# Dense-token operands written to DRAM by the routing step instead of transposed again by the dense step

## The chip, the core and the metric

The kernel runs on one core of one Trainium2 chip. The metric is the device time of one execution in microseconds (us), taken as the median of several runs. A further execution is recorded by the hardware profiler, and all durations below are from that one.

## What is computed

One layer of a transformer over 1024 latent tokens (8 blocks of 128) with 256 context tokens, width 1024. After a mixing half (retention and differential attention, not touched here) comes the expert half:

```python
x = x + mod[:, 2] * (jnp.concatenate([ret_lat, diff_lat], axis=-1) @ w_out[layer])
h2 = modulate(x, norm2_g[layer], mod[:, 3], mod[:, 4])
x = x + mod[:, 5] * peer_ffn(h2, peer_w_query[layer], peer_sub_keys[layer], peer_u[layer], peer_v[layer])

def block_fn(hb):                       # 128 tokens of h2
    q = (hb @ w_query).reshape(t, PEER_HEADS, 2, PEER_HALF)
    s = jnp.einsum('thpc,hpnc->thpn', q, sub_keys)
    v1, i1 = lax.top_k(s[:, :, 0], PEER_TOPK)
    v2, i2 = lax.top_k(s[:, :, 1], PEER_TOPK)
    ...
    u, vsel = expert_u[experts], expert_v[experts]
    act = jax.nn.gelu(jnp.einsum('thkd,td->thk', u, hb), approximate=False)
    return jnp.einsum('thk,thkd->td', gate * act, vsel)
```

Each token picks 16 of 16384 experts in each of 8 heads (routing) and adds up their outputs with gates.

## The kernel before

**Blocks.** The eight token blocks are mixed in five groups, `GROUPS = [[0], [4, 5], [6, 7], [3], [1, 2]]`. For each group, `mix` (attention, output projection, residual, second norm) leaves the normalised tokens `x1` in buffers of tag `b` (four buffers) and writes them to DRAM (`h2d[b]`). `route` then transposes the group's tokens on TensorE with the identity (`mm<-ident,b`), copies them to tiles `hts` (also tag `b`), and for each of the 8 heads loads the query weights (`wst<-w_query_chunks`, two of the four `wst` buffers), multiplies (`mm<-b,wst`), copies the queries (`u<-mm`), scores them against the keys (`mm<-sk,u`), and finds the 16 best on VectorE (`vi`, `s`), twice per block and head (once for each half key). `select` combines them.

**Two ways of evaluating the experts.** Blocks 0, 1 and 2 gather expert rows with indirect DMAs (`halves`: `gat<-peer_u`, `gat<-peer_v`, and a VectorE operation for each). Blocks `DENSE = [3, 4, 5, 6, 7]` (640 tokens) go through all 16384 experts in `dense_phase`. For these, `gates` first writes a table of gate values to DRAM (`Wd`): one unit of four tokens is a VectorE pair, four ScalarE operations `t<-ob,pt`, four TensorE multiplications `mm<-t,t` and four ScalarE copies (`rv<-mm` or `gat<-mm`). There are 160 units.

**The dense operands.** Products run as three multiplications of rounded halves (`three`), so the tokens are needed transposed, as a high half (five tiles of tag `k`) and a low half (five tiles of tag `v`), each 128 by 1024:

```python
ts = [sb([128, 1024], tag, F32R) for _ in range(5)]
wide = [ts[k // 2][:, k % 2 * 384:(k % 2 + 1) * 384] for k in range(KD)]
thin = [ts[k][:, 768:1024] if k < 4 else ts[4][:, (k - 4) * 256:(k - 3) * 256] for k in range(KD)]
```

`wide` holds blocks 3, 4, 5, `thin` blocks 6, 7. The same buffers hold keys and values of the attention until the last group has been mixed. `split_tokens` fills them: it loads `h2d` of each dense block (tag `b`), transposes it again (8 transposes for a block), and for each 128 by 128 piece ScalarE rounds the high half from PSUM and VectorE subtracts for the low half. Then `dense_act` loads the experts' columns (`wst<-peer_u_cols`), splits them (`h<-wst`, ScalarE then VectorE) and multiplies (`mm<-k,h`, `mm<-v,h`), and after four of these `dense_val` multiplies with the experts' output rows (`mm<-h,rv`, `mm<-h,t`).

**The order of the work.** Nothing is issued as it is written. Every operation is recorded as a node (all instructions therefore carry line L591, a helper's). Parts that shall overlap are interleaved by `weave`, which places operation j of n of a part at a fraction `lo + (hi - lo) * j / n`; the last weave joins `gates` of block 3, `dense_phase`, and `route` of blocks 1 and 2. Then `Plan.schedule` simulates the engines and the buffers by a table of costs and picks, on each engine, the ready node of lowest priority number whose buffers are free. It runs seven times with adjusted priorities, and the best order is built. So a change of one part's length or of its dependences can move instructions anywhere after it.

Of the kernel before, what the change touches and what calls it, by code (L numbers as in the profile page):

```python
# [6 lines left out]
F32 = mybir.dt.float32  # L7
# [5 lines left out]
OP = mybir.AluOpType  # L13
AX = mybir.AxisListType

D = 1024
# [5 lines left out]
KD = D // 128  # L22
# [38 lines left out]
DENSE = [3, 4, 5, 6, 7]  # L61
ND = 128 * len(DENSE)
RANGES = [(0, 384), (384, 640)]
# [534 lines left out]
def layer(tc, I, out, dbg=None):  # L598
# [3 lines left out]
    with sp as S, pp as P, dp as DR:  # L602
# [9 lines left out]
        nc = Plan(tc, pools, bufs, {"mm": RESERVE})  # L612

        def eng(pattern, i):
            return nc.gpsimd if pattern[i % len(pattern)] == "P" else nc.vector

        def sb(shape, tag, dt=F32):
            return nc.tile(shape, dt, tag)

        def ps(shape):  # L620
            return nc.tile(shape, F32, "mm")

        def dr(shape, name):
            return nc.tile(shape, F32, name, dram=True)

        def dump(name, sl, t):
            if dbg is not None and name in dbg:
                nc.sync.dma_start(dbg[name][sl], t)


        ident = sb([128, 128], "ident")
# [19 lines left out]
        def rstd(dst, mean):  # L651

            n = mean.free
            nc.vector.tensor_scalar(dst, mean, EPS, None, op0=OP.add)
            nc.gpsimd.tensor_tensor(out=dst, in0=dst, in1=mhalf[:, :n], op=OP.pow)
# [24 lines left out]
        def wstream(src, c0):  # L680

            w = []
            for i in range(2):
                t = sb([128, 4, 256], "wst")
                nc.sync.dma_start(t, src[c0 // 256, :, i * 4:(i + 1) * 4, :])
                w += [t[:, k, :] for k in range(4)]
            return w
# [103 lines left out]
        for a in range(2):  # L791
            nc.vector.tensor_tensor(out=dec[:, a], in0=cols[:, a, :, None].to_broadcast([128, 4, H]),
                                    in1=lg[:, a:a + 1, :].to_broadcast([128, 4, H]), op=OP.mult)
# [303 lines left out]
        def mod_row(i):  # L1097
            t = sb([128, D], "h")
            nc.sync.dma_start(t, modr[i:i + 1, :].to_broadcast([128, D]))
            return t  # L1100
# [6 lines left out]
        h2d = [dr([128, D], f"h2d{b}") for b in range(NB)]  # L1107
# [78 lines left out]
        def mix(grp):  # L1186

            cT = []
            for b in grp:
                attend(b, cT)  # L1190
            x1 = [sb([128, D], "b") for _ in grp]
            gate1 = mod_row(0)
            for ch in range(4):
                w = wstream(wo, ch * 256)
                for i, b in enumerate(grp):
                    pm = ps([128, 256])
                    with nc.unit():
                        for k in range(KD):
                            nc.tensor.matmul(pm, cT[i][:, k, :], w[k], start=(k == 0), stop=(k == KD - 1))
                    cs = slice(ch * 256, (ch + 1) * 256)  # L1200
                    nc.vector.tensor_tensor(out=x1[i][:, cs], in0=pm, in1=gate1[:, cs], op=OP.mult)
            shift2, gs2 = mod_row(1), mod_row(2)
            for i, b in enumerate(grp):
                xr = sb([128, D], "wst")
                nc.sync.dma_start(xr, I["x"][0, b * 128:(b + 1) * 128, :])
                eng(XE, b).tensor_tensor(out=x1[i], in0=x1[i], in1=xr, op=OP.add)
                nc.sync.dma_start(x1d[b], x1[i])
                dump("x1", (slice(b * 128, (b + 1) * 128), slice(None)), x1[i])
                ms = sb([128, 2], "m4")
                nc.scalar.activation(xr, x1[i], AF.Square, scale=1.0 / 32.0, accum_out=ms[:, 0:1])  # L1210
                rstd(ms[:, 1:2], ms[:, 0:1])
                nc.vector.scalar_tensor_tensor(x1[i], x1[i], ms[:, 1:2], gs2, op0=OP.mult, op1=OP.mult)
                eng(XE, b).tensor_tensor(out=x1[i], in0=x1[i], in1=shift2, op=OP.add)
                nc.sync.dma_start(h2d[b], x1[i])
                dump("h2", (slice(b * 128, (b + 1) * 128), slice(None)), x1[i])
            return x1

        def top16(i, h, qT, sk, v16, i16):
            pm = ps([128, 2, 128])
            for s in range(2):  # L1220
                nc.tensor.matmul(pm[:, s, :], qT[s][:, i, :], sk[:, s, :], start=True, stop=True)
            s0 = sb([128, 2, 128], "u3")
            nc.scalar.copy(s0, pm)
            for s in range(2):
                s1 = sb([128, 128], "s1")
                vv, ii = v16[:, h, s, :], i16[:, h, s, :]
                nc.vector.max(vv[:, 0:8], s0[:, s, :])
                nc.vector.max_index(ii[:, 0:8], vv[:, 0:8], s0[:, s, :])
                nc.vector.match_replace(s1, vv[:, 0:8], s0[:, s, :], LOWEST)
                nc.vector.max(vv[:, 8:16], s1)  # L1230
                nc.vector.max_index(ii[:, 8:16], vv[:, 8:16], s1)

        def route(grp, x1):
            T = len(grp)
            kpt = KD // T
            hts = [sb([128, kpt, T, 128], "b") for _ in range(T)]
            for i, b in enumerate(grp):
                for g in range(KD // 4):
                    tp = ps([128, 4, 128])
                    with nc.unit():  # L1240
                        for q in range(4):
                            k = g * 4 + q
                            nc.tensor.transpose(tp[:, q, :], x1[i][:, k * 128:(k + 1) * 128], ident)
                    k0 = (g * 4) % kpt
                    nc.scalar.copy(hts[g * 4 // kpt][:, k0:k0 + 4, i, :], tp)
            vi = [sb([128, 2, PH, 2, TK], "vi") for _ in grp]
            v16, i16 = [t[:, 0] for t in vi], [t[:, 1].bitcast(U32) for t in vi]
            for h in range(PH):
                w = wstream(wq, h * 256)
                sk = sb([128, 2, 128], "sk")  # L1250
                nc.sync.dma_start(sk, I["peer_keys_cols"][h])
                qT = []
                for s in range(2):
                    pm = ps([128, T * 128])
                    with nc.unit():
                        for k in range(KD):
                            nc.tensor.matmul(pm, w[k][:, s * 128:(s + 1) * 128],
                                             hts[k // kpt][:, k % kpt].rearrange("p t c -> p (t c)"),
                                             start=(k == 0), stop=(k == KD - 1))
                    q = sb([128, T, 128], "u0" if s else "u4")  # L1260
                    nc.scalar.copy(q.rearrange("p t c -> p (t c)"), pm)
                    qT.append(q)
                for i in range(T):
                    top16(i, h, qT, sk, v16[i], i16[i])
            for i, b in enumerate(grp):
                select(b, v16[i], i16[i])

        def split_tokens():

            parts = []  # L1270
            for tag in ("k", "v"):
                ts = [sb([128, 1024], tag, F32R) for _ in range(5)]
                wide = [ts[k // 2][:, k % 2 * 384:(k % 2 + 1) * 384] for k in range(KD)]
                thin = [ts[k][:, 768:1024] if k < 4 else ts[4][:, (k - 4) * 256:(k - 3) * 256] for k in range(KD)]
                parts.append([wide, thin])
            for i, b in enumerate(DENSE):
                x = sb([128, D], "b")
                nc.sync.dma_start(x, h2d[b])
                f = 0 if i < 3 else 1
                cs = slice(i * 128 - RANGES[f][0], (i + 1) * 128 - RANGES[f][0])  # L1280
                for g in range(KD // 2):
                    tp = ps([128, 2, 128])
                    with nc.unit():
                        for q in range(2):
                            k = g * 2 + q
                            nc.tensor.transpose(tp[:, q, :], x[:, k * 128:(k + 1) * 128], ident)
                    for q in range(2):
                        h_, l_ = (t[f][g * 2 + q][:, cs] for t in parts)
                        nc.scalar.copy(h_, tp[:, q, :])
                        nc.vector.tensor_tensor(out=l_, in0=tp[:, q, :], in1=h_.bitcast(F32), op=OP.subtract)  # L1290
            return parts

        def select(b, v16, i16):
# [257 lines left out]
        def Q(g):  # L1551
            return C(route, GROUPS[g], x1s[g])
# [8 lines left out]
        for i in range(1, len(GROUPS) + 1):  # L1561
            assert LATE[min(i, len(LATE)) - 1] >= sum(map(len, GROUPS[1:i + 1]))
            q = Q(i - 1)
            last = i == len(GROUPS)
            parts = [] if last else [(q, *QSPAN[i - 1]), (A(i), *ASPAN[i - 1])]
# [76 lines left out]
```

## Time and profile before

| | us |
|---|---|
| median of 3 runs (lowest, highest) | 3334.67 (3334.27, 3337.14) |
| the profiled execution's own time | 3333.26 |
| its span, first to last instruction | 3331.5 |
| TensorE (PE) busy | 3088.1 (93%) |
| VectorE (DVE) busy | 2635.5 (79%) |
| ScalarE (ACT) busy | 1341.7 (40%) |
| GpSimd (POOL) busy | 1146.8 (34%) |

Shares are of the span. The engines work side by side, so the busy times don't add up; what a stage costs is read from the waits in that stage. Matmuls are pipelined: a group of n reads shorter, divided by n, than the mean of one. A float32 multiplication of the program stands in the trace as two matmul records, a transpose and a product of rounded halves as one. PEclk is the clock granted to TensorE, 1.00 being 2.4 GHz and 0.50 being 1.2 GHz.

### The profile page before, as it was taken

The page shows a single profiled execution, that of the slowest core. Times are in us where ns is not written, and L with a number is a line of the kernel's source. Part 1 is how long each engine was busy: PE and PEld are TensorE (multiplying, and loading weights), DVE is VectorE, ACT ScalarE, POOL GpSimd, SP SyncE. Part 2 cuts the span into 40 slices and gives each one's busy share as a digit, 9 for nine tenths or more (in the row PEclk, how much of TensorE's full clock was granted, in tenths as well). Part 3 has the DMA queues.
Part 4 walks back from the last instruction along what each step waited for, and adds up shares of the span by engine and source line. Part 5 has one row for each costly group of instructions (what it writes and reads, how often), then busy time and mean ns, then how long its engine had stood idle before and what let it go on. Part 6 is the DMA issues. An engine that isn't in the chain of part 4 may idle for free.

```text
span 3331.5 us, 51447 instructions
## 1 busy us (share of the span) xinstructions
PE 3088.1 (93%) x18272; PEld 2710.2 (81%) x18272; DVE 2635.5 (79%) x5951; ACT 1341.7 (40%) x3553; POOL 1146.8 (34%) x1099
## 2 busy tenths in 40 slices
PE   6998887878888898899999999999999999999998
PEld 4998576656767786788889898989898988999897
DVE  3457547879988988578988887888888887889895
ACT  5342454424356899883322222222222222222221
POOL 0101111453441201103545453454445443545440
PEclk7999998989989999999999999999999999999999
DMA  5222655886586553646888888888889887888883
GB/s 187 96 78 76 231 187 186 280 316 229 196 276 204 196 184 108 213 157 220 307 308 290 308 293 293 282 307 300 306 296 313 303 298 274 296 307 300 303 295 121
DMA packets 314531, 809.68 MB, mean 243 GB/s; under 512 B 29313, under 2 KB 125593, under 8 KB 314274
## 3 DMA queue, kind: packets, MB, share of 16 engines
q1 hardware_dynamic: 203682, 403.70, 35.9%
q0 software_dynamic: 110592, 402.70, 34.7%
q8 instruction: 144, 2.36, 0.3%
q14 instruction: 113, 0.93, 0.1%
HBM read 745.46 MB, written 60.83 MB: 242 GB/s over the span
## 4 chain that ended last, share of the span: by engine, by line
PE 54%; DVE 10%; ACT 6%; issue 3%; DMA 2%; POOL 1%; DVEq 0%; POOLq 0%; SPq 0%; ACTq 0%
PE mm L591 54%; ACT t L591 2%; DVE sel L591 2%; DVE acc L591 2%; ACT rv L591 1%; DVE gat L591 1%; DVE t L591 1%; ACT gat L591 1%; DVE h L591 1%; DMA gat<-peer_v,egb 1%; POOL gat L591 1%; DVE vi L591 1%; ACT h L591 1%; DVE m L591 1%; DMA gat<-peer_u,egb 1%
## 5 line engine op out<-in xcount | busy, mean ns | idle before, releaser
L591 PE MATMUL mm<-k,h 128*128 128x384 f32 (+1 forms) x4096 | 918.5, 309 | 6.2 <-DVE h L591 4.7
L591 PEld LDWEIGHTS mm<-k,h 128*128 128x128 f32 x4096 | 697.5, 189 | 15.4 <-DVE h L591 5.4
L591 POOL DMA_INDIRECT gat<-peer_u,egb x368 | 474.0, 1288 | 555.4 <-DVE acc L591 341.4
L591 ACT CAST h<-wst 128x512 fp32r<-128x512 f32 (+1 forms) x384 | 286.0, 764 | 888.8 <-PE mm L591 854.1
L591 POOL DMA_INDIRECT gat<-peer_v,egb x377 | 463.5, 1229 | 521.8 <-DVE gat L591 267.5
L591 PE MATMUL mm<-v,h 128*128 128x384 f32 (+1 forms) x2048 | 630.6, 308 | 0.0
L591 PE MATMUL mm<-h,rv 128*128 128x512 f32 x2304 | 586.7, 395 | 2.6 <-DVE h L591 1.8
L591 PEld LDWEIGHTS mm<-h,rv 128*128 128x128 f32 x2304 | 422.9, 188 | 96.6 <-DVE h L591 2.6
L591 DVE SCALAR_TENSOR_TENSOR acc<-gat,act,acc 128x1024 f32<-128x1024 f32 x374 | 480.6, 1285 | 6.4 <-DMA gat<-peer_v,egb 5.0
L591 DVE TENSOR_TENSOR h<-wst,h 128x512 fp32r<-128x512 f32 (+1 forms) x384 | 329.8, 867 | 177.6 <-ACT h L591 91.2
L591 DVE SCALAR_TENSOR_TENSOR gat<-gat,h2t 128x1024 f32<-128x1024 f32 x368 | 450.5, 1229 | 17.5 <-DMA gat<-peer_u,egb 17.5
L591 PE MATMUL mm<-h,t 128*128 128x512 f32 (+1 forms) x1600 | 416.8, 391 | 1.8 <-DVE t L591 1.1
L591 PEld LDWEIGHTS mm<-v,h 128*128 128x128 f32 x2048 | 386.4, 189 | 8.4
L591 PEld LDWEIGHTS mm<-h,t 128*128 128x128 f32 x1600 | 295.1, 189 | 68.2 <-DVE t L591 2.4
L591 POOL TENSOR_TENSOR m<-m,mhalf 128x4 f32<-128x4 f32 (+1 forms) x78 | 73.0, 938 | 689.5 <-DVE m L591 674.4
L591 PE MATMUL mm<-b,wst 128*128 128x256 f32 (+1 forms) x1280 | 240.5, 343 | 2.5 <-DMA wst<-w_query_chunks 2.1
L591 PE MATMUL mm<-t,t 128*128 128x128 f32 x1280 | 193.6, 298 | 45.0 <-ACT t L591 38.5
L591 ACT ACTIVATE t<-ob,pt 128x128 f32<-128x128 bf16 x640 | 220.1, 419 | 21.5 <-DVE ob L591 10.7
L591 PEld LDWEIGHTS mm<-b,wst 128*128 128x128 f32 x1280 | 206.2, 194 | 27.3 <-DMA wst<-w_query_chunks 2.7
L591 PEld LDWEIGHTS mm<-t,t 128*128 128x128 f32 x1280 | 173.4, 198 | 67.3 <-ACT t L591 58.4
L591 DVE TENSOR_TENSOR b<-b,mm 128x512 f32<-128x512 f32 x248 | 165.8, 682 | 61.5 <-PE mm L591 60.9
L591 PE MATMUL mm<-t,h 128*128 128x256 f32 x992 | 187.2, 286 | 6.2 <-DVE aT L591 2.8
(239 smaller groups left out, 4454.2 us busy)
## 6 DMA issues: line engine op xcount, KB each, us to landing
wst<-peer_u_cols SPq DMA_DIRECT2D x128, 512.0 KB, 7.3
wst<-peer_v_halves SPq DMA_DIRECT2D x128, 512.0 KB, 4.7
wst<-w_query_chunks SPq DMA_DIRECT2D x80, 512.0 KB, 5.7
h<-Wd SPq DMA_DIRECT2D x64, 512.0 KB, 7.8
wst<-w_mod_chunks SPq DMA_DIRECT2D x48, 512.0 KB, 5.1
wst<-w_out_chunks SPq DMA_DIRECT2D x40, 512.0 KB, 5.4
Wd<-rv SPq DMA_DIRECT2D x40, 512.0 KB, 3.6
Wd<-gat SPq DMA_DIRECT2D x40, 512.0 KB, 4.7
```

The lines of the kernel that those rows point to most:

```text
L591: getattr(handles[n.eng], meth)(*[res(v) for v in a], **k)
```

## The change

`route` additionally writes the transposed tokens of the dense blocks, which it holds in `hts` for its own use, to a DRAM tensor `h2T` of five 128 by 1024 tiles in the layout of the `k` and `v` tiles. `split_tokens` loads these five tiles and splits each with one ScalarE and one VectorE operation. The dense blocks' `h2d` is no longer written.

```diff
-                nc.sync.dma_start(h2d[b], x1[i])
+                if b not in DENSE:
+                    nc.sync.dma_start(h2d[b], x1[i])
...
+        h2T = dr([5, 128, 1024], "h2T")
+
         def route(grp, x1):
...
                     nc.scalar.copy(hts[g * 4 // kpt][:, k0:k0 + 4, i, :], tp)
+            for i, b in enumerate(grp):
+                if b in DENSE:
+                    d = DENSE.index(b)
+                    c0 = d * 128 if d < 3 else (d - 3) * 128
+                    for h, t in enumerate(hts):
+                        k0 = h * kpt
+                        if d < 3:
+                            for j in range(kpt // 2):
+                                o = h2T[k0 // 2 + j, :, 0:768].rearrange("p (a c) -> p a c", a=2)
+                                nc.sync.dma_start(o[:, :, c0:c0 + 128], t[:, 2 * j:2 * j + 2, i, :])
+                        else:
+                            if k0 < 4:
+                                o = h2T[k0:k0 + 4, :, 768 + c0:768 + c0 + 128].rearrange("j p c -> p j c")
+                                nc.sync.dma_start(o, t[:, 0:4, i, :])
+                            if k0 + kpt > 4:
+                                o = h2T[4].rearrange("p (a c) -> p a c", a=4)[:, :, c0:c0 + 128]
+                                nc.sync.dma_start(o, t[:, kpt - 4:kpt, i, :])
...
         def split_tokens():
-            parts = []
+            parts, raw = [], []
             for tag in ("k", "v"):
                 ts = [sb([128, 1024], tag, F32R) for _ in range(5)]
+                raw.append(ts)
...
-            for i, b in enumerate(DENSE):
-                x = sb([128, D], "b")
-                nc.sync.dma_start(x, h2d[b])
-                f = 0 if i < 3 else 1
-                cs = slice(i * 128 - RANGES[f][0], (i + 1) * 128 - RANGES[f][0])
-                for g in range(KD // 2):
-                    tp = ps([128, 2, 128])
-                    with nc.unit():
-                        for q in range(2):
-                            k = g * 2 + q
-                            nc.tensor.transpose(tp[:, q, :], x[:, k * 128:(k + 1) * 128], ident)
-                    for q in range(2):
-                        h_, l_ = (t[f][g * 2 + q][:, cs] for t in parts)
-                        nc.scalar.copy(h_, tp[:, q, :])
-                        nc.vector.tensor_tensor(out=l_, in0=tp[:, q, :], in1=h_.bitcast(F32), op=OP.subtract)
+            for j, (h_, l_) in enumerate(zip(*raw)):
+                x = sb([128, 1024], "b")
+                nc.sync.dma_start(x, h2T[j])
+                nc.scalar.copy(h_, x)
+                nc.vector.tensor_tensor(out=l_, in0=x, in1=h_.bitcast(F32), op=OP.subtract)
             return parts
```

Because the scheduler builds the order, the change also moves other instructions. The two kernels' orders, with the numbers of the buffers, show three places. The first is TensorE just before the dense step, in the kernel before (a `t4`/`t7` row is a gate unit, `ident` a transpose of `split_tokens`, `b_13597` and `b_13607` the routed tokens of blocks 1 and 2, `k_`/`v_` the dense step):

```order
L591 MATMUL mm_14798<-t4_14791,t3_14770 128x128 x4
L591 MATMUL mm_14824<-ident_117,b_14458 128x128 x2
L591 MATMUL mm_14841<-b_13597,wst_14346 128x256 x4
L591 MATMUL mm_14873<-b_13607,wst_14349 128x256 x4
L591 MATMUL mm_14889<-ident_117,b_14776 128x128 x2
L591 MATMUL mm_14921<-sk_14835,u4_14883 128x128
L591 MATMUL mm_14940<-ident_117,b_14851 128x128 x2
L591 MATMUL mm_14985<-b_13597,wst_14754 128x256 x4
L591 MATMUL mm_15001<-b_13607,wst_14892 128x256 x4
L591 MATMUL mm_15019<-sk_14934,u0_15017 128x128
L591 MATMUL mm_15081<-k_14400,h_15045 128x384
```

The same place with the change (`b_13690` and `b_13695` are now the routed tokens):

```order
L591 MATMUL mm_14404<-b_13695,wst_14098 128x256 x4
L591 MATMUL mm_14426<-t4_14388,t3_14390 128x128 x4
L591 MATMUL mm_14641<-t4_14633,t3_14618 128x128 x4
L591 MATMUL mm_14648<-sk_14153,u0_14175 128x128
L591 MATMUL mm_14663<-b_13690,wst_14239 128x256 x4
L591 MATMUL mm_14688<-b_13695,wst_14431 128x256 x4
L591 MATMUL mm_14705<-sk_14656,u0_14658 128x128
L591 MATMUL mm_14743<-b_13690,wst_14700 128x256 x4
L591 MATMUL mm_14756<-sk_14710,u0_14715 128x128
L591 MATMUL mm_14766<-b_13695,wst_14703 128x256 x4
L591 MATMUL mm_14817<-sk_14761,u4_14780 128x128
L591 MATMUL mm_14828<-k_13755,h_14786 128x384
```

Rows that only continue a run are left out: between `mm_14426` and `mm_14641` stand 11 more gate units and nothing else. The last 13 units now stand alone, while before the transposes, heads and units alternate to the end; the transposes are gone; and two heads of blocks 1 and 2 follow the last unit in both. The second place is TensorE some 50 instructions into the dense step of the changed kernel; in the kernel before, nothing but the dense step's own multiplications stands there:

```order
L591 MATMUL mm_14832<-k_14089,h_14815 128x256
L591 MATMUL mm_14918<-sk_14822,u4_14846 128x128
L591 MATMUL mm_14923<-sk_14822,u0_14844 128x128
L591 MATMUL mm_14926<-k_13755,h_14819 128x384
L591 MATMUL mm_14951<-b_13690,wst_14808 128x256 x4
L591 MATMUL mm_14951<-b_13695,wst_14824 128x256 x4
L591 MATMUL mm_14981<-b_13690,wst_14808 128x256 x4
L591 MATMUL mm_14981<-b_13695,wst_14824 128x256 x4
L591 MATMUL mm_15007<-sk_14940,u4_14991 128x128
L591 MATMUL mm_14926<-k_13917,h_14819 128x384
```

The last head of the route of blocks 1 and 2 (16 multiplications) and eight score multiplications, four of them of the head ahead of it, have moved from before the dense step into it. The third place is the queue of SyncE, where blocks 4 and 5 pass from mixing to routing, first before and then with the change (`x1d` and `t2` belong to mixing, `wst` and `sk` are loads that route waits for):

```order
L591 DMA x1d5_6709<-b_6603 128x1024
L591 DMA wst_6715<-w_query_chunks 128x1024
L591 DMA t2_6738<-retd7_4339 128x512
L591 DMA h2d4_6780<-b_6541 128x1024
L591 DMA h2d5_6835<-b_6603 128x1024
L591 DMA wst_6890<-w_query_chunks 128x1024
L591 DMA wst_6898<-w_query_chunks 128x1024
L591 DMA sk_6921<-peer_keys_cols 128x256
```

```order
L591 DMA t2_6750<-retd7_4339 128x512
L591 DMA h2T_6864<-b_6812 128x2x128 x2
L591 DMA h2T_6864<-b_6816 128x2x128 x2
L591 DMA wst_6906<-w_query_chunks 128x1024
L591 DMA wst_6912<-w_query_chunks 128x1024
L591 DMA h2T_6864<-b_6812 128x2x128
L591 DMA sk_6923<-peer_keys_cols 128x256
L591 DMA h2T_6864<-b_6812 128x2x128
L591 DMA h2T_6864<-b_6816 128x2x128 x2
```

The whole writes of two blocks have become pieces that stand between the loads of the route's weights; over the program 16 such writes replace 5.

## Rows read from the trace of the kernel before

**Rows 1.** The page's first part: busy time of each engine over the span.
```profile
PE 3088.1 (93%) x18272; PEld 2710.2 (81%) x18272; DVE 2635.5 (79%) x5951; ACT 1341.7 (40%) x3553; POOL 1146.8 (34%) x1099
```
**Rows 2.** Busy time by stretch: stretch, length, engines (count), granted clock, DMA share, GB/s.
```profile
600.00:1341.80 741.80, 617.34 (x3506) 509.60 (x3506) 650.68 (x2036) 462.14 (x1485) 225.92 (x277) 0.92 0.64 219
1341.80:1393.30 51.50, 43.39 (x239) 38.50 (x237) 29.85 (x51) 37.73 (x133) 11.99 (x7) 0.93 0.66 227
1393.30:1494.90 101.60, 93.00 (x570) 83.71 (x571) 67.16 (x253) 88.66 (x348) 0.00 (x0) 1.00 0.48 163
1494.90:1521.10 26.20, 19.61 (x107) 16.67 (x105) 20.57 (x122) 11.45 (x43) 3.90 (x12) 0.97 0.93 327
1521.10:3294.50 1773.40, 1768.90 (x9863) 1596.91 (x9864) 1506.97 (x2434) 476.57 (x908) 823.94 (x674) 1.00 0.84 290
```
**Rows 3.** Waits of ScalarE in 1393.3 to 1494.9: total us, times, longest.
```profile
ACT u L591 <- PE mm L591: 8.6, 4, 3.5
ACT t L591 <- PE mm L591: 4.2, 5, 2.1
```
**Rows 4.** Timeline of TensorE, gates with the routing of blocks 1 and 2: start, us, operation.
```profile
1407.48 1.39 PE L591 MATMUL mm<-t,t 128*128 128x128 f32 x8 [0.31 <-ACT t L591]
1409.50 1.39 PE L591 MATMUL mm<-t,t 128*128 128x128 f32 x8 [0.63 <-ACT t L591]
...
1420.81 7.07 PE L591 MATMUL mm<-b,wst 128*128 128x256 f32 x32
1427.71 1.95 PE L591 MATMUL mm<-t,t 128*128 128x128 f32 x16
...
1431.29 10.53 PE L591 MATMUL mm<-b,wst 128*128 128x256 f32 x48
```
**Rows 5.** Timeline of TensorE just before the dense step.
```profile
1502.55 1.04 PE L591 MATMUL mm<-ident,b 128*128 128x128 f32 x8
1503.42 1.06 PE L591 MATMUL mm<-sk,u 128*128 128x128 f32 x8
```
**Rows 6.** Timelines of ScalarE and VectorE there: splits of tokens and of experts' columns.
```profile
1503.07 1.46 ACT L591 CAST k<-mm 128x128 fp32r<-128x128 f32 x8
...
1514.66 2.94 ACT L591 CAST h<-wst 128x1024 fp32r<-128x1024 f32 x3
```
**Rows 7.** ScalarE groups in 1393.3 to 1494.9: busy us, mean ns, idle before.
```profile
L591 ACT COPY u<-mm 128x256 f32<-128x256 f32 x22 | 8.9, 420 | 8.6 <-PE mm L591 8.6
```
**Rows 8.** The chain that ended last, 1492 to 1524: start, us, what.
```profile
1501.01 6.57 DMA wst<-w_query_chunks
...
1519.77 1.27 DVE h L591
```
**Rows 9.** Timeline of VectorE: first and last operation of two searches for 16 best.
```profile
1505.17 0.48 DVE L591 MAX8 vi<-u 128x8 f32<-128x128 f32 x2
...
1509.65 0.28 DVE L591 FIND_INDEX8 vi<-vi,u 128x8 uint32<-128x128 f32 x1
```
**Rows 10.** Groups of instructions over the span: table loads and the gathers' sums.
```profile
L591 DVE SCALAR_TENSOR_TENSOR acc<-gat,act,acc 128x1024 f32<-128x1024 f32 x374 | 480.6, 1285 | 6.4 <-DMA gat<-peer_v,egb 5.0
...
L591 ACT ACT_TABLE_LOAD x28 | 35.9, 1283 | 8.2 <-DVE sel L591 4.5 <-DMA rgd<-fin 2.1 <-PEq L1631 0.7
```
**Rows 11.** DMA issues: count, KB each, median us to landing.
```profile
h<-Wd SPq DMA_DIRECT2D x64, 512.0 KB, 7.8
...
h2d<-b SPq DMA_DIRECT2D x8, 512.0 KB, 3.1
```
**Rows 12.** Splits and transposes in 1341 to 1522: busy us, mean ns, idle before.
```profile
L591 PE MATMUL mm<-ident,b 128*128 128x128 f32 x56 | 9.9, 313 | 0.1
...
L591 DVE TENSOR_TENSOR v<-mm,k 128x128 fp32r<-128x128 f32 x40 | 9.1, 280 | 1.7 <-ACT k L591 1.7
```
**Rows 13.** Busy time by stretch: gate units alone, and the dense step's first 4.9 us.
```profile
1408.00:1420.00 12.00, 8.21 (x49) 7.03 (x49) 6.71 (x12) 12.00 (x49) 0.00 (x0) 1.00 0.50 200
1521.10:1526.00 4.90, 4.90 (x18) 4.90 (x19) 4.90 (x29) 0.00 (x0) 4.74 (x14) 0.50 0.73 226
```

## The prediction, made before the changed kernel was run

> **What bounds the kernel now.** I read the busy times first, then the same by stretch, then in each stretch the waits, and the timelines where a wait needed a name. TensorE is busy 93% of the span [rows 1], but not evenly. From 1521.1 us, where the dense step gets going, to 3294.5 it is busy 1768.9 of 1773.4 us [rows 2]. That stretch holds the dense step's multiplications and nothing else on TensorE, it is the same work after the change, and every microsecond that TensorE spends there on something else is paid in full. So two questions decide: when does the dense step start, and what foreign work is in it. Ahead of it no single engine is full: from 600 to 1341.8, where the last attention ends, VectorE is busy 650.7 of 741.8 us, and TensorE 617.3; then TensorE and ScalarE take turns [rows 2]. The work of `split_tokens` lies between 1393 and 1521, among the gates of block 3 and the routing of blocks 1 and 2.
>
> **What is removed, by itself.** 40 transposes: eight in a row take 1.04 us [rows 5], so 0.13 each, 5.2 us of TensorE. (Their mean of 313 ns [rows 12] overlaps the neighbours, so it isn't the price.) 40 ScalarE roundings at 1.46/8 = 0.18 each become five of 1024 columns at 2.94/3 = 0.98 each [rows 6]: 7.2 against 4.9 us. VectorE's 40 subtractions of 9.1 us together [rows 12] become five at up to 1.27 [rows 8], 6.4 us. The last two save 2 to 3 us on each engine.
>
> The Trainium skill prices a transpose otherwise: "TensorE: Matmul & The Clock Gate", section "Part 4: PE-mode transpose", has about 275 ns for one inside a kernel, most of it access latency. An estimate from that page makes the removal 11 us instead of 5.2. The rows agree with it as a duration of one, and not as a price in a run of eight.
>
> **The writes and loads.** SyncE gets 16 writes of 128 or 256 KB in pieces of 512 bytes for five whole ones. No row has such a write. The nearest are the whole write, landing after 3.1 us, and the load of `Wd`, which is in pieces of 512 bytes too and takes 7.8 [rows 11]. Between these ends it makes no difference to the sum: the pieces are read only shortly before the dense step, most of them long after they are written, and `hts` stays held anyway until the eight heads are done. What stands behind them on SyncE's queue are the route's weights, and they are fetched ahead. I cost it at nothing; if that cover went, each group of writes would hold the next weights by at most 7.8 us, once for each of the three dense groups.
>
> **Where the order moves: 1393.3 to 1494.9** (to the last gate unit, 101.6 us). ScalarE waits there for TensorE 8.6 + 4.2 = 12.8 us [rows 3] and works 88.8. By the order listing it now has 18 roundings less (3.2 us), 11 query copies less at 8.9/22 = 0.40 [rows 7] (4.5) and one gate unit less (2.0, the pace of units alone [rows 4]), and five long roundings more (4.9): 84.0 us, the lower bound if it never waits; with all of its waits 96.8. The waits come where TensorE runs 32 or 48 records of routing in one go, 7.07 and 10.53 us [rows 4]. The new order has no run above 16. It has about 25 units mixed with 160 routing records and 20 score records, then 13 units alone. TensorE's part of the mix is 25 x 1.95/2 + 160 x 10.53/48 + 20 x 1.06/8 [rows 4, 5] = 62.1 us, ScalarE's about 60; the 13 units take 13 x 2.02 = 26.3. That gives 88.4, and with a few mutual waits I take **91, so 10.6 earlier**, between 17.6 and 4.8.
>
> **From the last unit to the dense step** (26.2 us now [rows 2]). In the new order: 4 score records (0.5), a head of 32 records at 0.22 (7.0). The next head's weights need a buffer that the first head frees at about 5.8; the load takes 6.57 [rows 8], so it lands at 12.4, with TensorE idle since 8.6. Half a head (3.5) and its scores (1.1) end at 17.0, the copy at 17.4; VectorE then searches twice at (1509.65 + 0.28 - 1505.17)/2 = 2.4 [rows 9] and subtracts the first low half, 1.27 [rows 8]: 23.5. I take **2.7 earlier**. If the weights come early, VectorE's chain alone binds, five searches and the subtraction, 13.2 with 0.9 ahead of it, 12 earlier than now; if they come later, nothing is gained.
>
> **In the dense step.** The last routing head (32 records, 7.0 us) and eight score multiplications (16 records, 2.1 us) now stand inside it, **9.1 later**, with little doubt. Its other additions (searches on VectorE) fit: two searches and a subtraction are 6.1 us, and TensorE has two expert columns in hand, 96 records, at the stretch's pace of 1773.4/9863 = 0.18 us [rows 2] some 17 us.
>
> **Before 1341.8.** The instructions are the same, but the order is built anew. The listings show four more ScalarE table loads, 1.28 us each, and four more gather operations on VectorE of 1.29 us [rows 10] ahead of the last attention, 10.2 us together. ScalarE is idle 280 of these 741.8 us and VectorE 91 [rows 2], so most is hidden: between 0 and 10.2, I take 1. A reordering as such can also gain or lose several microseconds which no row can tell; it is in the range, not in the sum.
>
> **Sum.** -10.6 - 2.7 + 9.1 + 1 = -3.2 us on the profiled execution, 3333.26 to 3330.1. The median shown, 3334.67, is 1.4 above that execution, so I forecast **3331.5**, in other words: the transposes' time is gained, and some of it is lost to idle time of an order that is not better. A measurement of this kernel can tell about 0.2%, 6.7 us, from no change; this is below it.
>
> **Rivals.**
> - *The mix closes up* (faster). ScalarE hardly waits (17.6 earlier), the weights are there in time (another 5 or so beyond my 2.7, 7.7 in all): -17.6 - 7.7 + 9.1 + 1 = -15.2, 3319.5. For it: no long run is left. Against: the four buffers for weights, two of which the experts' columns take. It tells from the point where the dense step starts 17 us earlier. Chance 0.25.
> - *Transposes cost what one takes* (faster). They stand singly between other work, and 40 x 0.313 [rows 12] = 12.5 us go instead of 5.2: 7.3 more, 3324.2. Against: TensorE's timeline has no gap around them. Chance 0.08. The Trainium skill's page on TensorE named above, taken at its word, says this too.
> - *The moved head is paid and the start doesn't come* (slower). Place: the last head, inside a stretch where TensorE is full. Price 9.1. If the gates alone at the end keep the last unit where it was and the weights come late, the start moves by 0 to 2.4 us and the kernel is 6.7 to 9.1 slower, up to 3343.8. The point is a dense start less than 2.4 us earlier. For it: 13 units alone leave TensorE half idle, where now it has transposes and heads to do. Against: ScalarE has less to do in all. Chance 0.14.
> - *The time before moves* (slower). The table loads and gathers land on the chain that ends the last attention, 10.2 instead of 1: +6.0, and more with the reordering, 3341 to 3346. Chance 0.11.
> - *The clock falls during the units alone* (near no change). The first head after them would run at half clock, 7.0 more: 3338.5. Against: twelve microseconds of units alone kept 1.00, while the dense step's first 4.9 us, after a wait, were granted 0.50 [rows 13]. Chance 0.08. The Trainium skill, "TensorE: Matmul & The Clock Gate", section "Part 1: The HAM clock gate", says that throttled is the default and that activity lifts it; by that rule a half idle TensorE speaks against this change.
> - *Nothing takes effect*: the splits were hidden and stay so, and only the order's noise is left; that is within the forecast's band and cannot be told from it by time.
>
> **How the numbers follow.** The forecast has 0.34, and with the clock's rival 0.42 lie within 0.2%. Faster by more: 0.25 + 0.08 = 0.33. Slower by more: 0.14 + 0.11 = 0.25. The likeliest case alone spans 3328 to 3338. The range takes in most of the mix that closes up and of the late start: 3317 to 3345.
>
> **What would show it.** Right: the dense step's first product some 13 us earlier than 1521, TensorE full from there, 48 more routing and score records inside it, no token transposes for it, ScalarE's waits for TensorE between the last attention and the last gate well under 12.8. Wrong: a last attention that ends more than 5 us away from 1341.8, gaps in the dense step, or weights for the last heads that arrive later than said.

## The result: 32 us slower, and the profile after

| | before | after |
|---|---|---|
| median, us (4 runs each) | 3334.47 | 3366.22 (3361.72 to 3371.66) |
| the profiled execution: own time, span | 3333.26, 3331.5 | 3361.72, 3360.0 |
| ratio, 95% interval | | 1.0091 [1.0076, 1.0106] |

The change costs 32 us. The forecast was 3331.5, the range ended at 3345, and no rival reached 3366. The first view is the busy time by stretch of the changed kernel (columns as in [rows 2]).

```profile
600.00:1333.50 733.50, 623.01 (x3515) 514.16 (x3514) 645.35 (x2035) 471.74 (x1496) 235.05 (x278) 0.91 0.64 223
1333.50:1392.00 58.50, 47.66 (x255) 42.03 (x253) 33.64 (x54) 38.70 (x140) 13.02 (x7) 0.85 0.56 194
1392.00:1485.00 93.00, 80.92 (x486) 72.91 (x487) 56.60 (x158) 86.49 (x319) 0.00 (x0) 0.98 0.53 184
1485.00:1509.26 24.26, 19.46 (x95) 16.53 (x94) 13.16 (x82) 7.66 (x23) 0.00 (x0) 0.93 0.71 229
1509.26:3322.98 1813.72, 1782.15 (x9911) 1604.60 (x9911) 1517.16 (x2527) 479.73 (x914) 800.46 (x681) 0.99 0.83 284
3322.98:3360.00 37.02, 28.15 (x122) 22.37 (x120) 22.99 (x39) 3.58 (x8) 0.00 (x0) 0.95 0.44 142
```

Its bounds are the same events as before: the last value product of the attention (its end, 1340.9 before, by TensorE's timeline; the prediction had set this bound at 1341.8), the first routing product of blocks 1 and 2 (1393.3), the last gate unit, the dense step under way, its end. So the prediction's steps can be set beside what happened, in us:

| step | before | after | change | predicted |
|---|---|---|---|---|
| start to the last attention | 1340.9 | 1333.5 | -7.4 | +1 |
| from there to the routing of blocks 1 and 2 | 52.4 | 58.5 | +6.1 | 0 |
| gates with that routing | 101.6 | 93.0 | -8.6 | -10.6 |
| last gate to the dense step under way | 26.2 | 24.3 | -1.9 | -2.7 |
| dense step | 1773.4 | 1813.7 | **+40.3** | +9.1 |
| tail | 37.0 | 37.0 | 0 | 0 |

The sum is +28.5, the difference of the spans. The dense step does start 11.8 us earlier, nearly as predicted (12.3). Everything is lost inside it. TensorE's waits there (operations, total us, times, longest), first before (the 4.7 ended just as the step got going), then after (its first 1.25 likewise):

```profile
PE mm L591 <- DVE h L591: 6.5, 3, 4.7
PE mm L591 <- DVE t L591: 1.1, 3, 0.7
PE mm L591 <- DVE rv L591: 0.7, 1, 0.7
PE mm L591 <- DVE b L591: 0.7, 1, 0.7
```
```profile
PE mm L591 <- DVE h L591: 15.1, 7, 8.5
PE mm L591 <- ACT rv L591: 5.8, 1, 5.8
PE mm L591 <- DVE t L591: 5.5, 4, 3.4
PE mm L591 <- DVE rv L591: 5.3, 4, 2.9
PE mm L591 <- DVE b L591: 1.0, 1, 1.0
```

Inside the step that is 31.4 us instead of 4.3, 27.1 more. TensorE's timeline of the changed kernel shows where, and the foreign work:

```profile
1516.02 1.05 PE L591 MATMUL mm<-sk,u 128*128 128x128 f32 x8
...
1518.66 7.07 PE L591 MATMUL mm<-b,wst 128*128 128x256 f32 x32
1525.57 0.38 PE L591 MATMUL mm<-sk,u 128*128 128x128 f32 x2
...
1527.56 0.83 PE L591 MATMUL mm<-sk,u 128*128 128x128 f32 x6
...
1555.23 1.22 PE L591 MATMUL mm<-h,rv 128*128 128x512 f32 x2 [5.84 <-ACT rv L591]
1559.30 3.35 PE L591 MATMUL mm<-h,rv 128*128 128x512 f32 x7 [2.85 <-DVE rv L591]
...
1621.22 1.47 PE L591 MATMUL mm<-h,t 128*128 128x512 f32 x4 [3.44 <-DVE t L591]
1636.20 4.80 PE L591 MATMUL mm<-h,rv 128*128 128x512 f32 x14 [8.50 <-DVE h L591]
```

The moved head and scores take 7.07 + 1.05 + 0.38 + 0.83 = 9.3, as predicted (9.1). Around the two groups of waits TensorE has a lower granted clock, a mix of its two levels (0.50 and 1.00):

```profile
1555.00:1570.00 15.00, 10.98 (x35) 7.83 (x36) 14.96 (x29) 4.59 (x9) 6.81 (x7) 0.70 0.82 272
1621.00:1640.00 19.00, 10.27 (x31) 7.86 (x32) 18.96 (x34) 4.49 (x10) 12.76 (x11) 0.73 0.84 277
```

An estimate from these rows is 0.30 x 10.98 + 0.27 x 10.27 = 6.1 us of slow work, less the 2.5 (half of 4.9) that the kernel before loses at its start [rows 13]: 3.6. Together 27.1 + 9.3 + 3.6 = 40.0 of the 40.3. (TensorE's busy time in the step rose by 13.2, from 1768.9 to 1782.2; less the 9.3 that is 3.9 of slower work, close to the estimate.) What TensorE waited for at 1555 stands in the timelines of VectorE and ScalarE, behind its first value product:

```profile
1545.73 2.25 PE L591 MATMUL mm<-h,rv 128*128 128x512 f32 x9
```
```profile
1534.88 0.32 DVE L591 MAX8 sel<-sel 128x8 f32<-128x50 f32 x2
...
1551.98 0.99 DVE L591 TENSOR_REDUCE sel<-sel 128x16 f32<-128x800 f32 x1
...
1553.35 0.69 DVE L591 TENSOR_TENSOR h<-wst,h 128x512 fp32r<-128x512 f32 x1
...
1554.29 0.28 DVE L591 TENSOR_TENSOR aT<-aT,t 128x128 f32<-128x128 f32 x1
```
```profile
1554.66 0.51 ACT L591 CAST rv<-aT 128x384 fp32r<-128x384 f32 x1 [0.88 <-DVE aT L591]
```

`select` of the first block runs from 1534.9 to 1553.4 in one piece. The split of the experts' rows (`h`) and the product `aT`, which ScalarE rounds to `rv`, come behind it, and TensorE has stood since 1549.4 for them. In the kernel before, the same piece lies at 1523 to 1541, right behind the first three columns' splits, while TensorE multiplies these columns; it needs the first values only at 1551:

```profile
1523.32 0.31 DVE L591 MAX8 sel<-sel 128x8 f32<-128x50 f32 x2
...
1539.96 0.98 DVE L591 TENSOR_REDUCE sel<-sel 128x16 f32<-128x800 f32 x1
```
```profile
1551.33 2.26 PE L591 MATMUL mm<-h,rv 128*128 128x512 f32 x9
```

So counted from the dense step's start (1521.1 and 1509.3) the selection began 2 us behind it before, and begins 26 us behind it now.

### The profile page after: what moved, and what is told of

It reads as the page before. It is cut to its first block, busy times and chain, and to the rows that moved or that the text cites. A ratio compares the mean times of both kernels' runs of the same rounds, so it can differ in the third digit from the quotient of the medians.

```text
span 3360.0 us, 51334 instructions
## 1 busy us (share of the span) xinstructions
PE 3096.9 (92%) x18232; PEld 2712.3 (81%) x18232; DVE 2630.2 (78%) x5916; ACT 1346.4 (40%) x3522; POOL 1133.4 (34%) x1099
## 5 line engine op out<-in xcount | busy, mean ns | idle before, releaser
L591 POOL DMA_INDIRECT gat<-peer_u,egb x369 | 463.0, 1255 | 559.4 <-DVE acc L591 298.8
L591 POOL DMA_INDIRECT gat<-peer_v,egb x373 | 451.0, 1209 | 492.6 <-DVE gat L591 263.2
L591 PE MATMUL mm<-h,rv 128*128 128x512 f32 x2304 | 592.8, 398 | 24.3 <-DVE h L591 13.1
L591 PE MATMUL mm<-t,t 128*128 128x128 f32 x1280 | 200.8, 306 | 47.8 <-ACT t L591 29.3
L591 PEld LDWEIGHTS mm<-t,t 128*128 128x128 f32 x1280 | 180.6, 207 | 69.8 <-ACT t L591 52.1
```

Source lines behind the costliest of these rows:

```text
L591: getattr(handles[n.eng], meth)(*[res(v) for v in a], **k)
```

## The experiments

Medians and ratios are against the kernel before, run on the same chip beside it. I began with theory W: the weave counts operations, and with 110 fewer in `split_tokens` the dense step's first column falls to fraction 0.0212 instead of 0.0296, ahead of the end of the routing (0 to 0.05).

**The place in the weave.** The first run puts the changed kernel's fraction back, the second gives the kernel before the changed one's, the fourth goes beyond; the third adds the writes alone.

```diff
-DSPAN = [0.02, 0.0, 0.05]
+DSPAN = [0.0285, 0.0, 0.05]    e1: changed kernel
+DSPAN = [0.0115, 0.0, 0.05]    e2: kernel before
+DSPAN = [0.032, 0.0, 0.05]     e4: changed kernel
```

> The changed kernel with the dense step's place in the last weave moved from 0.02 to 0.0285, so that the first expert column again gets the fraction that it had before the change (0.0296, where the change made it 0.0212); nothing else is edited. Theory W (the weave counts operations: with 110 fewer of them ahead, the dense step outranks the end of the routing of blocks 1 and 2, and VectorE does that routing's searches and selection where the dense step needs its splits): no routing or score multiplication inside the dense step, TensorE's waits in it about 9 us as before instead of 32.7, time 3322 to 3336, so level with the kernel before or up to 12 us faster. Rival D (the new data path itself is slow: pieces of 512 bytes, or splits of whole tiles): 3355 to 3370 as the change had. Rival N (any new order costs or gains tens of us by luck): anywhere from 3310 to 3370, and no relation to what stands inside the dense step.

Measured: 3363.21, 1.0086 [1.0072, 1.0100]. No routing stands inside the dense step, which has its old length (1778 us from its first product), and yet nothing is won. The loss has moved ahead of the step, to its first product, which waits for ScalarE, which stands at an exponential of `select` until VectorE's selection is done (timelines of TensorE and ScalarE):

```profile
1540.97 0.69 PE L591 MATMUL mm<-k,h 128*128 128x384 f32 x1 [27.16 <-ACT h L591]
```
```profile
1539.67 0.31 ACT L591 ACTIVATE sel<-sel 128x128 f32<-128x128 f32 x1 [23.88 <-DVE sel L591]
1539.89 2.92 ACT L591 CAST h<-wst 128x1024 fp32r<-128x1024 f32 x3
```

> The kernel before with the dense step's place in the last weave moved from 0.02 to 0.0115, so that its first expert column gets the fraction that the change gave it (0.0212); transposes, loads and everything else as before. Theory W: the loss of the change without the change: the last routing head and score multiplications inside the dense step, TensorE's waits there 20 us or more, time 3350 to 3375. Rival D: 3325 to 3340, since the data path is the old one. Rival N: anything between, without the waits for VectorE's splits.

Measured: 3361.59, 1.0079 [1.0064, 1.0094]; waits in the dense step 23.2 us. As theory W said.

> The changed kernel with the dense step's place in the last weave moved from 0.02 to 0.032, beyond the place that it had before the change. Theory W: like the run with 0.0285, since the routing ends ahead of the dense step in both, 3320 to 3338. Rival D: 3355 to 3370. Rival N: it differs from the run with 0.0285 by 10 us or more in either direction.

Measured: 3359.39, 1.0070 [1.0055, 1.0086], with a wait of 22.8 us for VectorE's split that ends at 1545.25, early in the step. Not as theory W said.

> The kernel before with the 16 writes of the transposed tokens added in route and nothing read from them: the dense step still loads and transposes. Theory W: the last weave is unchanged, so no routing multiplication stands inside the dense step and the time stays within 10 us of before, 3328 to 3345; what the writes do to the order before the last attention is seen alone (with the change the last attention ended 8 us earlier). Rival D, if the writes are what costs: 3355 to 3370, with late query weights. Rival N: anywhere from 3310 to 3370.

```diff
+            h2T written from hts as in the change; h2d still written, loaded and transposed
```

Measured: 3369.26, 1.0100 [1.0085, 1.0116], the last attention 16 us later than before and 24.6 us of waits in the dense step. Theory W falls: four orders, with and without routing in the dense step, lose 25 to 35 us each. So the next question was whether the path or the order costs, and they had to be separated.

**Path and order exchanged.** These kernels plan one program and build the other in its order. Every operation gets a key (its part and its number in it) that the change leaves alone; `place` sorts by the other plan's position. The first loop takes the operations that both programs have, the second a split, a load or a write that only one has (`t` is its time in the other plan, `low` the place behind what it depends on; `...` marks lines left out):

```python
for n in self.nodes:
    if n.key[0] == "c" and n.key in rank:
        i = rank[n.key]
        at[n.seq] = (i, 0, 0)
...
for n in self.nodes:
    if n.seq not in at:
        ...
        at[n.seq] = max((bisect.bisect_right(starts, t) - 1, 1, n.seq), (low[0], 1, n.seq))
return sorted(self.nodes, key=lambda n: at[n.seq])
```

> The changed kernel's operations in the order of the kernel before, instruction by instruction on every engine: the order is planned for the old program, the operations that both have keep their places, each of the five loads and five roundings and subtractions takes the place of the last one of the block that it replaces, and the writes of the transposed tokens are issued as soon as the copies that they read are done. Theory O (what the change removes is worth something, and all of the loss comes from the order that the planner builds anew, in which the work of routing meets the splits of the dense step on VectorE and ScalarE): 3322 to 3335, a gain of up to 12 us from the 40 transposes (5.2 us of TensorE) and ScalarE's saved copies. Theory W (only the dense step's place in the last weave): the same, but then the run with that place put back should have been fast, which it was not. Rival D (the new data path itself is slow): 3355 to 3370.

> The kernel before, instruction by instruction in its own order, with nothing added but the 16 writes of the transposed tokens on SyncE's queue, each issued as soon as the copies that it reads are done; nothing reads what they write. Theory O: 3332 to 3340, the writes are free, and the 3369 of the kernel with the writes in a newly planned order was the order's. Rival D, the writes hold up the query weights behind them on the queue: 3355 to 3370, with waits for these weights of 10 us and more.

> The opposite exchange: the kernel before's operations (whole writes, loads, 40 transposes, roundings and subtractions by piece) in the order that the planner built for the changed kernel, the pieces of a block at the place of the changed kernel's rounding. Theory O: as slow as the change or a little slower, 3360 to 3380. Rival D: 3330 to 3345.

```diff
-PASSES, SHARES = 7, (0.3, 0.5)
+PASSES, SHARES = 4, (0.3, 0.5)    e8: kernel before
```

> The kernel before with nothing changed but the number of the planner's passes, four instead of seven, so that the order of the fourth pass is built instead of that of the sixth: the same instructions in another order. Theory O, in its strong form (the order of the kernel before is a lucky one among its like, and nearly any other costs some 25 to 35 us, as the four orders tried so far did): 3350 to 3375. In its weak form (the orders differ by 10 us or so, and what the change meets is special): 3330 to 3347. Rival D says nothing of it.

| ratio [95% interval] | old order | new order |
|---|---|---|
| old path | 1 | e7: 1.0125 [1.0105, 1.0145], 3374.80 us |
| old path and the writes | e6: 0.9999 [0.9989, 1.0009], 3335.33 us | |
| new path | e5: 1.0018 [1.0009, 1.0027], 3341.27 us | the change: 1.0091 [1.0076, 1.0106] |

By the ratios the order costs 42 us with the old path and some 24 with the new one; the writes cost nothing; the path costs 6 us in the old order and saves 11 in the new one (an estimate from the two intervals: between 3 and 20). With the transposes back, the new order shows the change's waits again, nearly one by one (waits of TensorE in the dense step, e7):

```profile
PE mm L591 <- DVE h L591: 14.5, 6, 8.7
PE mm L591 <- ACT rv L591: 6.1, 1, 6.1
```

And e8, the kernel before with not one instruction changed, only in the order of another pass, took 3352.58, 1.0048 [1.0032, 1.0063], with 22.5 us of such waits. The dense step in its trace, counted from its first product, is 15.8 us longer than before (1794.5 for 1778.7), as much as the ratio says. That lies just inside the range of theory O's strong form, though below its 25 to 35 us: each new order of the planner tried so far costs 16 to 42 us. But e5, at 3341, missed theory O's 3322 to 3335 by 6 us.

**The 6 us of e5.** SyncE's queue, e5 first, then before:

```profile
1503.82 0.33 SPq L591 DMA_DIRECT2D b<-h2T  x1
...
1505.74 1.05 SPq L591 DMA_DIRECT2D sk<-peer_keys_cols  x1
```
```profile
1491.51 0.41 SPq L591 DMA_DIRECT2D b<-h2d  x1
...
1496.80 0.77 SPq L591 DMA_DIRECT2D sk<-peer_keys_cols  x1
```

The fourth load needs a buffer of tag `b`, which with the new path is free only after VectorE's subtraction. It stands at the head of the queue for it, and the keys behind it come late (e5: SyncE's waits from 1440 to 1525, then TensorE just before the dense step):

```profile
SPq L591 <- DVE v L591: 9.8, 2, 8.3
```
```profile
1512.53 2.05 PE L591 MATMUL mm<-sk,u 128*128 128x128 f32 x8 [5.79 <-DMA sk<-peer_keys_cols]
```

> The changed kernel's operations in the order of the kernel before, as in the run of that name, but each of the five tiles is rounded and subtracted as soon as its load has landed, some 60 to 100 us earlier, and the next load follows as soon as its buffer is free; in the earlier run each stood at the place of the last piece of the old block. There the fourth load waited for its buffer, held SyncE's queue, and the keys for the last heads came late (a wait of 5.8 us on TensorE just before the dense step). If that is what made the change 6 us slower in the old order: no such wait, the dense step 5 to 9 us earlier relative to the last attention, 3328 to 3336. Rival: the 6 us come from somewhere else on the way (the writes, or the order of ScalarE in the gates), and the time stays at 3339 to 3344.

Measured: 3334.53, 0.9995 [0.9986, 1.0004]. The wait is gone and so are the 6 us. With nothing in its way, the new path is worth between 5 us gained and 1 us lost.

**What in the order.** Around the start of the dense step VectorE has become the fullest engine; 1507 to 1660, before and after:

```profile
1507.00:1660.00 153.00, 144.01 (x805) 130.28 (x804) 138.31 (x374) 50.87 (x90) 69.50 (x91) 0.98 0.76 260
```
```profile
1507.00:1660.00 153.00, 129.84 (x702) 114.94 (x702) 142.95 (x411) 44.64 (x82) 72.16 (x95) 0.93 0.73 249
```

> The changed kernel in its own order, with TensorE's and SyncE's orders untouched, and one thing moved: the selection of the experts of blocks 1 and 2 (its operations on VectorE, with ScalarE's exponentials and GpSimd's share) stands 25 us of the plan later, behind the first values' splits of the dense step, among its operations instead of ahead of them. Theory O, in its particular form (what the new order pays for is the 18 us of selection that VectorE does at 1535 to 1553 while TensorE waits for the splits behind it, and again at 1605 to 1636): TensorE's waits in the dense step fall from 32.7 to 10 to 20 us, and the time from 3366 to 3340 to 3356. Rival P (the waits come from the whole load on VectorE in these 150 us, wherever the selection stands, or from late expert rows): the waits stay at 28 to 35, the time at 3360 to 3372.

Measured: 3381.84, 1.0133 [1.0118, 1.0149], 15 us slower than the change. The first wait shrank (5.84 to 1.1 us, at 1552), but others came: 7.4 at 1563, 6.0 at 1579, 7.6 at 1635, 10.1 at 1652, in all

```profile
PE mm L591 <- DVE h L591: 17.9, 8, 10.1
PE mm L591 <- DVE t L591: 15.8, 4, 7.6
PE mm L591 <- DVE rv L591: 10.1, 5, 6.0
```

Theory O's particular form falls, and rival P, which had the waits unchanged, is too kind: VectorE, whose order now mixes selection and splits, stood still itself for other engines (7.4 us in one wait for ScalarE, 7.0 in two for GpSimd; busy 123 instead of 143 of the 153 us) and had the selection still to do.

> The changed kernel in its own order, instruction by instruction, with VectorE's sums over gathered expert rows cut from 1024 to 32 columns for those planned from 20 us before to 150 us after the start of the dense step (some 35 to 40 of 1.25 us each, so about 45 us of VectorE; this leaves out most of the products of these rows). Theory P (VectorE is simply full there, 143 of 153 us between 1507 and 1660, whatever stands ahead of what): TensorE's waits in the dense step fall from 32.7 to under 15, the second group of them, at 1615 to 1636, above all; time 3340 to 3352. Theory O in its particular form, the selection alone: the waits at 1549 to 1564 stay (some 10 us), the others halve; 3350 to 3360. Rival (late data, not VectorE's work): waits of 28 and more, time as the change.

```diff
+                    if meth == "scalar_tensor_tensor" and n.thin:
+                        a = [x[:, 0:32] if i in (0, 1, 3) else x for i, x in enumerate(a)]
```

Measured: 3354.62, 1.0058 [1.0043, 1.0074], 12 us faster than the change. TensorE's waits:

```profile
PE mm L591 <- DVE egb L591: 6.0, 1, 6.0
PE mm L591 <- ACT rv L591: 6.0, 1, 6.0
PE mm L591 <- DVE h L591: 5.1, 5, 2.0
```

They fall to 21.6. The wait behind the first selection (`ACT rv`) stays at 6.0; the 3.4 + 8.5 later on, where sums over gathered rows stand among the second block's selection, shrink to 6.0 (`DVE egb`). In these last 6.0, from 1629.6 to 1635.6, VectorE hardly selects: it waits itself for gathered rows, 2.3 us and 1.8 us, the first being

```profile
1631.10 0.19 DVE L591 SCALAR_TENSOR_TENSOR gat<-gat,h2t 128x32 f32<-128x32 f32 x1 [2.33 <-DMA gat<-peer_u,egb]
```

So no theory has it alone, and the time fits the second (the selection) better: the sums had some 11 us of the waits, 6 us stay right behind a selection, and the other 6 lie mostly behind rows that land late.

The other orders' traces say more for the selection. VectorE's operations on `sel` fill 20.0 of the longest wait of 27.2 us in e1, 9.7 of 10.8 in e2, 11.6 of 13.5 in e3, 18.6 of 22.9 in e4 and 10.2 of 12.1 in e8. In the change they fill 3.9 of the first long wait of 5.8, but 1.2 of the longest, 8.5, in which sums over gathered rows have 5.2.

> The changed kernel in an order put together from two: up to the end of the last attention the order that the planner built for the changed kernel (its last attention ended 7 us earlier, at 1333 instead of 1340, also with the old transposes in that order), and from there the order of the kernel before, with the five tiles split as soon as they are loaded. If each part keeps what it showed by itself, this is the fastest: 3324 to 3332, with TensorE's waits in the dense step at 9 to 11 us. If the early gain belongs to what that order leaves for later, it comes out at 3332 to 3342.

Measured: **3329.61, 0.9979 [0.9970, 0.9988]**, 7 us faster than the kernel before and 37 faster than the change, with the same operations as the change. The waits in the dense step are the old ones (10.3 from its first product, where the kernel before has 10.5). It has the change's own order up to the last attention, so the loss sits behind that point. Its trace is of an execution of 3336.74, so it doesn't show where the last 5 us against e10 come from.

## Why the prediction was wrong

**The step that failed** is "In the dense step": "Its other additions (searches on VectorE) fit". It counted two searches and a subtraction, 6.1 us, against 17 us in hand. It left out what follows the last head: `select` needs all eight heads, so when the last head moves into the dense step, the whole selection of the block moves behind it, 18 us on VectorE in one piece, and the sums over gathered rows follow. The order listing that showed the moved head showed TensorE; VectorE's rows behind it were not followed. That is the term: 40.3 us where 9.1 stood. The moved head itself cost its 9.3; 27.1 are waits that the sum had at nothing, and 3.6 the lower clock around them. That these come with the order and not with the new path is shown (e5, e7, e10, e12). How much of them is the selection's is not settled: moving it later alone made things worse (e9), and thinning the sums took 11 us off (e11).

**The rivals.** "The moved head is paid and the start doesn't come" had the place and the 9.1 right, the start wrong (it came 11.8 us earlier), and the price too small by the same omission. "The clock falls" was put into the units alone; there it fell a little (0.98 in 1392 to 1485; one run of 24 records of units, at 1471.55, took 5.39 us, where 24 at 1350.69 took 3.06), but the head behind them kept its 7.07 us. It fell further in the dense step around the waits, to 0.70 and 0.73, some 4 us. The Trainium skill, "TensorE: Matmul & The Clock Gate", section "Part 1: The HAM clock gate", has the clock throttled unless activity lifts it; the two rows agree with that. "The mix closes up" and "The time before moves" did not come: the dense step started 11.8 us earlier, not 17, and the last attention ended earlier, not later (the 10.2 of that step add up to 10.3, which changes nothing). Two of the prediction's own signs of being wrong came: the last attention more than 5 us away, and gaps in the dense step.

**The steps that held.** Gates with routing: -8.6 for -10.6; ScalarE waits there for TensorE 3.6 us (2.0 and 1.6) instead of 12.8 [rows 3]. Last unit to the dense step: -1.9 for -2.7. Writes at nothing: e6. The loads, at nothing too, cost 6 us through SyncE's queue in e5; in the change's own order no run separates them. That the dense step starts as early as said is in part luck, since two errors nearly cancel: the last attention 7.4 us earlier, and the output projection behind it 6.1 longer, in which TensorE was busy at a granted clock of 0.85, where it had 0.93 before [rows 2].

**The transposes.** The 5.2 us of TensorE count for little: at equal order (e10) the new path gives 1.4 us less by the medians, between 4.7 less and 1.3 more by the interval. From the last attention to the dense step under way, the kernel before, then e10:

```profile
1340.90:1521.10 180.20, 156.90 (x922) 139.78 (x921) 117.99 (x428) 138.74 (x524) 15.89 (x19) 0.98 0.60 204
```
```profile
1346.10:1526.30 180.20, 155.53 (x882) 139.04 (x880) 116.03 (x393) 136.89 (x490) 15.88 (x19) 0.94 0.60 204
```

The stretch is as long without the 40 transposes as with them. TensorE's busy time falls by 1.4 us and not by 5.2: the granted clock is lower, so by an estimate from these rows 3.8 come back as slower multiplications, and the 1.4 are idle time. Another pair has the same (e6 0.97, e12 0.94, both 179.5 us), and e5, with the splits at their old places, has 0.94 too. The Trainium skill, "TensorE: Matmul & The Clock Gate", section "Part 4: PE-mode transpose", has about 275 ns for one; an estimate from it, 11 us for 40, lies outside that interval.

**"A reordering as such can also gain or lose several microseconds"**: it was put into the time before the last attention only, at a few us. It was the largest term of the change, and behind that point.

## What to carry to other kernels

Where a planner builds the order, the time of a small edit is the edit plus a new order, and the second part can be larger by far: build the new program in the old order (and the old in the new) before judging the edit. When an operation moves into a stretch where one engine is full, follow its results on the other engines as far as they go; here the price stood on another engine. And a load that waits for a buffer holds everything behind it on its queue, so whatever frees the buffer should come as early as its data allow.

## What was not expected

The same order ends its first part at quite different times. Up to the last attention the change, e7, e9 and e11 have the same order on TensorE, and the last value product ended at 1333.5, 1333.0, 1336.6 and 1341.6 us; e12, whose order on TensorE is the same for the first 7345 of the 7369 records up to there, had 1346.2. The old order spreads as widely: 1340.9 before, 1344.2 in e5, 1337.6 in e6 and 1346.1 in e10. So the -7.4 in the table above may be no effect of the new order at all: a difference of 8 us there in a single trace says nothing. That the dense step's waits depend so strongly on the order of VectorE's work was not expected either: 10 us to 45 us of them, with the same instructions.

What stays open: which order behind the last attention would be best. One that moves a single part (e1, e4, e9) lost each time; nothing was tried that plans this part anew with VectorE's true load.
